# Down projection of a hybrid encoder's feed-forward layer: 18 of 22 inner tiles by seven products instead of 12, and the last 512 tokens finished in two parts

## The chip, the cores and the metric

The kernel runs on one core of one Trainium2 chip. The metric is the device time of one execution in microseconds; several executions are timed, and their median counts. One further execution was taken with the hardware profiler, and all rows quoted below come from it. The engines are TensorE (PE, with its weight loads as PEld), VectorE (DVE), ScalarE (ACT), GpSimd (POOL) and SyncE (SP), which issues most of the DMAs.

## What is computed

One layer of an encoder on 1024 tokens of width 1024, in float32: two token mixers side by side, then a gated feed-forward layer, then a final RMSNorm. The change concerns the end:

```python
def _conv_glu_ffn(h, w_up, dw_w, dw_b, w_down):
    up = jnp.einsum("bsd,df->bsf", h, w_up)
    gate, val = jnp.split(up, 2, axis=-1)
    gate = _dwconv_centred(gate, dw_w, dw_b)
    return jnp.einsum("bsf,fd->bsd", jax.nn.silu(gate) * val, w_down)
...
x = x + _conv_glu_ffn(h2, ...)
...
return _rmsnorm(x, final_norm_w)
```

The inner width is 2816, that is 22 tiles of 128. The down projection multiplies a matrix of 1024 tokens x 2816 by one of 2816 x 1024.

## The kernel before

**Layout.** Activations lie with channels on the 128 partitions and tokens along them. A page is 128 x 512 float32: one tile of 128 channels for one half (512) of the tokens. An output column tile `i` (0 to 7) has two pages, `xr[i][0]` and `xr[i][1]`.

**A product in full precision** (`mm3`, lines 142 to 150) is three matmuls: every operand is split (`split`, line 122) into a high part, cast by ScalarE, and the rest, subtracted by VectorE (both appear as line 124 in the profile); high x high, high x low and low x high are added up in PSUM. Lines 148, 149 and 150 are these three.

**Seven products** (`pair_job`): two output tiles (`i` and `i + 4`) x two token halves are a 2 x 2 block of a product whose inner tiles are also taken as two halves of `NS` = 3. Such a block takes seven products of `NS` inner tiles instead of eight, with sums of operands and of weights as inputs. The sums of activations (four per pair of inner tiles, `g_sums`) are made in the up stage and stored in `d_gc`; the sums of weights are either made in the job by four additions (`plus`, line 312) or made ahead once in `down_sums` (line 1945), stored in `d_ws` and read back. A job of seven products runs in the order 1, 2, 6, 7, 5, 4, 3; each product is issued in two steps, so a job has 14 steps (`per_seven`). After products 1, 6 and 7 `take` (line 1807) adds what `xr` held; after 2, 5, 4 and 3 `f` in `seven_evac` (line 1811) writes the new value of one page.

**Stages of the down projection.** `FIRST` = 6 inner tiles go through plain jobs (`std_down`), one job per output tile, two halves each, two inner tiles a step, 6 steps a job; ScalarE copies the result into `xr` (line 1797). Then `SEVENS` = 2 groups of 6 inner tiles by seven products, four jobs each. In the last group, when a page gets its final value of that group, POOL issues a DMA that adds the residual `d_x2` onto it (line 1814). Then the 4 remaining inner tiles (`LAST0` and up) in 16 plain jobs (`last_jobs`), all eight tiles for the first 512 tokens, then all eight for the last 512. After each, VectorE adds the result to `xr` (line 1869) and `turn_out` is issued four steps later: TensorE turns the page into token order, four blocks of 128 x 128 (line 1882), ScalarE takes squares with their sum (line 1884), VectorE multiplies by the gain into a separate tile `y` (line 1893). When all eight tiles of a half are there, the sums are reduced (1889), scaled (1890) and raised to -1/2 by POOL (1891), and `scale_out` multiplies each block of 128 tokens by its factor, 640 columns on VectorE (1917) and 384 on ScalarE (1914), and stores it (1920).

**Order.** TensorE runs in program order, which is written out by hand. `run_jobs` yields after each step; a job's weights are prepared one job ahead by a generator that pauses for a number of steps (`yield 4` and so on) between loads and splits; whatever is not ready when a product needs it is issued at that point. `later(n, do)` issues `do` after `n` further steps. The other engines and queues are ordered by a planner, but for instructions marked `pin`, which stay behind all that was issued before them on their engine. `fill_to(n)` runs steps up to number `n`; the lists `at` say at which step each operand of the next group is loaded (`load_seven`, line 1760; it is split four steps later). Operands take two pages out of 48 (`hx`, 32, and `gx`, 16) in turn, a group of seven needs 42. PSUM has three banks `mm`, two `sc`, two `tr` and one `ob`. Loaded weights pass through `wr` (two buffers, line 135) into `wp` (four).

The up stage before it (`ffn_job`) also runs by seven products; after each inner tile `gated` makes the gated value and stores it in `d_g`.

Of the kernel before, what the change touches and what calls it, by code (L numbers as in the profile page):

```python
# [30 lines left out]
BASE_STEPS = 1  # L31
H = 512
# [15 lines left out]
def tile_hybrid_encoder(  # L48
# [500 lines left out]
    def scratch(name, *dims):  # L549
# [1055 lines left out]
    ffn_order = [*range(FIRST), *in_pairs, *range(LAST0, NF)]  # L1605
    b12_only = in_pairs[::2]
# [18 lines left out]
    def ffn_job(n):  # L1625
# [3 lines left out]
        def gated(hf):  # L1629
# [146 lines left out]
    for half in range(2):  # L1776
# [4 lines left out]
    advance_chores(1 << 10)  # L1781
# [4 lines left out]
    xr = [[page(fd, "xr", 2 * ND) for _ in range(2)] for _ in range(ND)]  # L1786
    fnw = fd.tile([P, D], F32, name="fnw")
    nc.sync.dma_start(
        fnw, bass.AP(tensor=final_norm_w.tensor, offset=final_norm_w.offset, ap=[[0, P], [1, D]])
    )  # L1790
# [4 lines left out]
    def first_evac(i):  # L1795
# [3 lines left out]
        return f  # L1799

    def seven_evac(i, last):
# [7 lines left out]
        def f(e, half, x0, x1=None, op=ALU.add):  # L1809
            t = out_of(e, half)  # L1810
            V.tensor_tensor(t, x0, t if x1 is None else x1, op=op)
            if last:
                o = i + e * ND // 2
                G.dma_start(t, d_x2[o][half], accum_op=ALU.add)
# [11 lines left out]
    def seven_down(s):  # L1826
# [18 lines left out]
        return [job(i) for i in range(ND // 2)]  # L1845

    def last_jobs(f0, evac):

        kept = {}

        def job(i, half):
            def prep():
                if i not in kept:
                    raw = raw_w(w_cols(ffn_w_down, f0 * P, 4, i * P), 4)
                    pages = [g_page().rearrange("p (k e) -> p k e", k=4) for _ in range(2)]
                    kept[i] = split(*pages, raw, V)
                return kept[i]

            return prep, std_job(None, 4, lambda k, h: gs[f0 + k, h], evac(i), (half,), 1)[1]

        return [job(i, half) for half in range(2) for i in range(ND)]

    y_tags = itertools.cycle(["tr", "sc"])

    def final_evac(i):


        def f(half, acc):
            V.tensor_tensor(xr[i][half], acc, xr[i][half], op=ALU.add)
            later(4, lambda: turn_out(i, half))  # L1870

        return f

    def turn_out(i, half):

        t = xr[i][half]
        if i == 0:
            out_y.append(fy.tile([P, 4, D], F32, tag="y", name=nm("y"), bufs=2))
        ss, y = out_ss[half], out_y[half]
        b = bank(next(y_tags))  # L1880
        for c in range(4):
            T.transpose(b[:, c * P : (c + 1) * P], t[:, c * P : (c + 1) * P], ident)
        for c in range(4):
            A.activation(
                out_junk[c % 2], b[:, c * P : (c + 1) * P], AF.Square, accum_out=ss[:, i, c : c + 1]
            )
        if i == ND - 1:
            rs = cp.tile([P, 4], F32, name=nm("frs"), tag="frs", bufs=2)
            V.tensor_reduce(rs, ss.rearrange("p i c -> p c i"), axis=AX.X, op=ALU.add)
            V.tensor_scalar(rs, rs, 1.0 / D, EPS, op0=ALU.mult, op1=ALU.add)  # L1890
            G.tensor_tensor(rs, rs, mhalf.to_broadcast([P, 4]), op=ALU.pow)
            out_r.append(rs)
        gain = V.tensor_tensor(
            y[:, :, i * P : (i + 1) * P],
            b.rearrange("p (c e) -> p c e", c=4),
            view(fnw, i * P, [[0, 4], [1, P]]),
            op=ALU.mult,
        )
        if i == ND - 1:
            pin(gain)  # L1900

    def finish(half):
        for c in range(4):
            if half == 0:
                later(2 * c + 3, lambda c=c: scale_out(half, c))
# [3 lines left out]
    def scale_out(half, c):  # L1909
        y, rs = out_y[half], out_r[half]  # L1910
        for o, cols in ((0, 640), (640, D - 640)):
# [117 lines left out]
```

## Time and profile before

| | |
|---|---|
| runs | 1744.45, 1746.06, 1745.98 us |
| median | 1745.98 us |
| profiled execution | 1742.35 us |
| its span, first to last instruction | 1740.5 us |
| TensorE busy in the span | 98% |
| VectorE, ScalarE, POOL busy | 72%, 48%, 10% |
| moved by DMA | 308.26 MB, 177 GB/s |

In rows of the time order the columns are start in us, duration in us, engine, line, operation, output <- inputs, partitions x elements, number of instructions merged, and in brackets the idle time before it and what ended it. In rows of groups they are line, engine, operation, names, shapes, number | busy us, mean ns of one | idle us before, by releaser. `SPq` is the queue of DMA issues on SyncE. Matmuls are pipelined: the duration shown of one is longer than the time from its start to the next.

### The profile page before, as it was taken

The page shows a single profiled execution, that of the slowest core. Times are in us where ns is not written, and L with a number is a line of the kernel's source. Part 1 is how long each engine was busy: PE and PEld are TensorE (multiplying, and loading weights), DVE is VectorE, ACT ScalarE, POOL GpSimd, SP SyncE. Part 2 cuts the span into 40 slices and gives each one's busy share as a digit, 9 for nine tenths or more (in the row PEclk, how much of TensorE's full clock was granted, in tenths as well). Part 3 has the DMA queues.
Part 4 walks back from the last instruction along what each step waited for, and adds up shares of the span by engine and source line. Part 5 has one row for each costly group of instructions (what it writes and reads, how often), then busy time and mean ns, then how long its engine had stood idle before and what let it go on. Part 6 is the DMA issues. An engine that isn't in the chain of part 4 may idle for free. (4 is left out here: it accounts for less than half of the span.)

```text
span 1740.5 us, 30439 instructions
## 1 busy us (share of the span) xinstructions
PE 1711.8 (98%) x11806; PEld 1409.4 (81%) x11806; DVE 1254.2 (72%) x1919; ACT 828.0 (48%) x1544; POOL 170.2 (10%) x184
## 2 busy tenths in 40 slices
PE   8999999999999999999999999999999999999997
PEld 6878888887888888888878887888888888888775
DVE  4599999746678888787556467667767776657864
ACT  7444433334476777776342245444334434443333
POOL 2211111100000000000000002011111111000110
PEclk9999999999999999999999999999999999999999
DMA  8768888855663444446589466577777776783842
GB/s 284 241 169 186 198 189 195 210 162 159 211 202 108 126 131 126 126 120 202 176 257 329 140 206 193 146 146 167 157 167 160 180 170 152 230 264 109 202 91 97
DMA packets 343750, 308.26 MB, mean 177 GB/s; under 512 B 25262, under 2 KB 255798, under 8 KB 343606
## 3 DMA queue, kind: packets, MB, share of 16 engines
q1 hardware_dynamic: 289590, 267.51, 49.0%
q0 software_dynamic: 44800, 37.76, 15.2%
q10 hardware_dynamic: 9216, 1.05, 0.4%
q8 instruction: 92, 1.51, 0.4%
q14 instruction: 52, 0.43, 0.1%
HBM read 201.40 MB, written 87.03 MB: 166 GB/s over the span
## 5 line engine op out<-in xcount | busy, mean ns | idle before, releaser
L148 PE MATMUL mm<-hx,wp 128*128 128x512 f32 x1068 | 427.3, 400 | 3.3 <-ACT tm L849 1.4
L150 PE MATMUL mm<-hx,wp 128*128 128x512 f32 x1068 | 417.1, 391 | 0.9 <-DVE wp L124 0.9
L149 PE MATMUL mm<-hx,wp 128*128 128x512 f32 x1068 | 416.6, 390 | 0.4 <-DVE hx L124 0.4
L124 ACT CAST wp<-wr 128x1024 fp32r<-128x1024 f32 (+2 forms) x147 | 147.2, 1002 | 258.6 <-PE mm L149 112.5
L148 PEld LDWEIGHTS mm<-hx,wp 128*128 128x128 f32 x1068 | 200.6, 188 | 46.7 <-DVE ev L798 2.2
L150 PEld LDWEIGHTS mm<-hx,wp 128*128 128x128 f32 x1068 | 200.4, 188 | 45.1 <-DVE wp L124 2.4
L149 PEld LDWEIGHTS mm<-hx,wp 128*128 128x128 f32 x1068 | 200.8, 188 | 40.5 <-DVE hx L124 1.2
L124 DVE TENSOR_TENSOR wp<-wr,wp 128x1024 fp32r<-128x1024 f32 (+2 forms) x145 | 169.5, 1170 | 67.3 <-ACT wp L124 61.0
L1037 DVE SCALAR_TENSOR_TENSOR acc<-gl,v_b,acc 128x1024 f32<-128x1024 f32 x120 | 149.2, 1282 | 0.4
L1142 DVE TENSOR_TENSOR qF<-qF,tb 128x512 f32<-128x512 f32 x96 | 65.1, 686 | 21.0 <-ACT A L1174 20.9
L439 ACT COPY su<-mm 128x512 f32<-128x512 f32 x82 | 47.5, 579 | 59.2 <-PE mm L150 58.9
L124 ACT CAST wq<-sw 128x1024 fp32r<-128x1024 f32 x41 | 43.1, 1052 | 59.5 <-PE mm L149 44.6
L148 PE MATMUL tr<-hx,wp 128*128 128x512 f32 x180 | 70.5, 392 | 0.0
L150 PE MATMUL tr<-hx,wp 128*128 128x512 f32 x180 | 70.1, 389 | 0.0
L149 PE MATMUL tr<-hx,wp 128*128 128x512 f32 x180 | 70.0, 389 | 0.0
L1634 DVE SCALAR_TENSOR_TENSOR tm<-gp,v_a,tm 128x512 f32<-128x512 f32 x88 | 66.0, 750 | 3.9 <-ACT tm L1632 2.0
L1142 DVE TENSOR_TENSOR kG<-kG,tb 128x512 f32<-128x512 f32 x96 | 65.3, 686 | 3.7 <-PE sc L1279 3.6
L148 PE MATMUL mm<-hy,wp 128*128 128x512 f32 x164 | 64.5, 393 | 0.0
L148 PE MATMUL sc<-hy,wq 128*128 128x512 f32 x164 | 64.3, 392 | 0.0
L149 PE MATMUL mm<-hy,wp 128*128 128x512 f32 x164 | 64.3, 392 | 0.0
L150 PE MATMUL sc<-hy,wq 128*128 128x512 f32 x164 | 64.2, 391 | 0.0
L149 PE MATMUL sc<-hy,wq 128*128 128x512 f32 x164 | 63.8, 389 | 0.0
(372 smaller groups left out, 3577.6 us busy)
## 6 DMA issues: line engine op xcount, KB each, us to landing
wr<-in_w_in_dram SPq DMA_DIRECT2D x48, 512.0 KB, 4.7
wr<-in_ffn_w_up_dram SPq DMA_DIRECT2D x22, 512.0 KB, 4.0
sw<-in_w_in_dram SPq DMA_DIRECT2D x38, 256.0 KB
d_g<-ft SPq DMA_DIRECT2D x38, 256.0 KB, 3.4
sw<-in_ffn_w_up_dram SPq DMA_DIRECT2D x38, 256.0 KB, 4.4
sw<-in_ffn_w_up_dram POOLq DMA_DIRECT2D x19, 512.0 KB, 8.1
wr<-sw POOLq DMA_DIRECT2D x32, 256.0 KB, 3.6
wr<-wr POOLq DMA_DIRECT2D x32, 256.0 KB, 4.0
```

The source lines that it names most:

```text
L124: parts = A.copy(hi, src), eng.tensor_tensor(lo, src, hi.bitcast(F32), op=ALU.subtract)
L148: T.matmul(acc, whi[:, k, :], ahi, start=first, stop=False, skip_group_check=again)
L149: T.matmul(acc, whi[:, k, :], alo, start=False, stop=False, skip_group_check=again)
L150: T.matmul(acc, wlo[:, k, :], ahi, start=False, stop=last, skip_group_check=again)
L439: A.copy(t, acc)
L1037: V.scalar_tensor_tensor(acc, g[:, k : k + S], tap(k), acc, op0=ALU.mult, op1=ALU.add)
L1142: V.tensor_tensor(o, a, b, op=op)
L1634: V.scalar_tensor_tensor(c, g[:, o + k : o + k + H], vec("fdw", k * NF + j), c, op0=ALU.mult, op1=ALU.add,)
```

## The change

The constants become `FIRST` = 4, `SEVENS` = 3, and the plain last tiles go. The third group does output tiles 0, 1, 2 and 4, 5, 6 by seven products; tiles 3 and 7 are done by plain jobs over its six inner tiles, the first 512 tokens at once, the last 512 in two parts of 256. The pages of tiles in the third group are turned as soon as they have their value, within the group, and the gained values go back into the page that held them (now parts of one tile `x_out[half]` each). The residual is added in four batches during the first group. Stored weight sums are for the first two jobs of the third group only. Loads are placed by one sorted list `plan`.

```diff
+STORED = ((2, 0), (2, 1))
...
-    FIRST, NS, SEVENS = 6, 3, 2
-    LAST0 = FIRST + 2 * NS * SEVENS
+    FIRST, NS, SEVENS = 4, 3, 3
     d_ws = {
-        si: dp.tile([P, 4, NS * P], F32, name="d_ws_%d_%d" % si) for si in ((0, 0), (0, 3), (1, 0))
+        si: dp.tile([P, 4, NS * P], F32, name="d_ws_%d_%d" % si) for si in STORED
     }
...
-    ffn_order = [*range(FIRST), *in_pairs, *range(LAST0, NF)]
-    b12_only = in_pairs[::2]
+    ffn_order = [*range(FIRST), *in_pairs]
+    b12_only = in_pairs[: 2 * NS * (SEVENS - 1) : 2]
...
-            if hf and FIRST <= j < LAST0:
+            if hf and j >= FIRST:
...
-    xr = [[page(fd, "xr", 2 * ND) for _ in range(2)] for _ in range(ND)]
+    x_out = [fd.tile([P, ND, H], F32, name=nm("xo")) for _ in range(2)]
+    xr = [[x_out[half][:, i, :] for half in range(2)] for i in range(ND)]
...
+    def residual(i):
+        for o in (i, i + ND // 2):
+            for half in range(2):
+                G.dma_start(xr[o][half], d_x2[o][half], accum_op=ALU.add)
...
             if last:
                 o = i + e * ND // 2
-                G.dma_start(t, d_x2[o][half], accum_op=ALU.add)
+                later(3, lambda: turn_out(o, half, range(4), "mm" if (e, half) == (1, 0) else "ob"))
...
-        return [job(i) for i in range(ND // 2)]
+        return [job(i) for i in range(ND // 2 - (s == SEVENS - 1))]
...
+    PARTS = [(0, range(4)), (1, range(2)), (1, range(2, 4))]
+    def last_jobs(f0):
+        tiles = ND // 2 - 1, ND - 1
+        def operand(k, half):
+            if half == 0:
+                return gs[f0, 1 + k // NS, k % NS]
+            return gs[f0 + k, 1] if k < NS else gs[f0, 3, k - NS]
+        def job(i, half, chunks):
+            cols = slice(chunks[0] * P, (chunks[-1] + 1) * P)
+            def steps(w):
+                raw = raw_w(w_cols(ffn_w_down, f0 * P, 2 * NS, i * P), 2 * NS)
+                yield 5 if i < ND // 2 else 3
+                w[0] = split(w_page(2 * NS), w_page(2 * NS), raw, V, True)
...
+                acc = bank("mm")[:, cols]
+                for k in range(2 * NS):
+                    act = [part[:, cols] for part in operand(k, half)]
+                    mm3(acc, w, act, k, k == 0, k == 2 * NS - 1)
+                    yield
+                t = xr[i][half][:, cols]
+                V.tensor_tensor(t, acc, t, op=ALU.add)
+                later(4, lambda: turn_out(i, half, chunks, next(y_tags)))
+        return [job(i, *part) for part in PARTS for i in tiles]
...
         gain = V.tensor_tensor(
-            y[:, :, i * P : (i + 1) * P],
+            t[:, o : o + n].rearrange("p (c e) -> p c e", e=P),
...
     def scale_out(half, c):
+        y = fy.tile([P, D], F32, tag="y", name=nm("y"), bufs=6)
+        r = out_r[half, c]
+        for i, m in ((0, 5), (5, 3)):
+            src = x_out[half][:, i : i + m, c * P : (c + 1) * P]
...
         if s == 0:
-            at = [12 + 2 * n for n in range(12)] + [starts[0] - 8 + n // 2 for n in range(6)]
-            at += [starts[0] - 5 + n for n in range(3)]
+            at = [8 + 4 * n // 3 for n in range(15)] + [starts[0] - 3 + n for n in range(3)]
+            at += [starts[0] + 1 + 2 * n for n in range(3)]
...
+    plan.append((starts[0] + 24, 1, lambda: load_gain))
+    for i, n in enumerate((18, 32, 60, 68)):
+        plan.append((starts[0] + n, 1, lambda i=i: lambda: residual(i)))
+    for k in range(NS):
+        at = starts[SEVENS - 1] + per_seven + 6 * k
+        plan.append((at, 4, lambda k=k: load_g(f0 + k, 1)))
+    for n, delay, do in sorted(plan, key=lambda p: p[0]):
+        fill_to(n)
+        later(delay, do())
...
+    fill_to(starts[SEVENS] + per_half + 3)
+    finish(*PARTS[0])
+    fill_to(starts[SEVENS] + 2 * per_half + 5)
+    finish(*PARTS[1])
     st.drain()
     advance_chores(1 << 10)
-    finish(1)
+    finish(*PARTS[2], late=False)
```

`turn_out`, the reduction and `finish` now take the blocks of 128 tokens they are to treat, so that each of the three parts has its own factors. The gain of the final norm is loaded during the first group instead of ahead of the stage. In place of one flush of pending work at the end of the up stage there is a loop, since the last pair's sums are now issued by work that is itself pending there.

More of the change, by code (lines that the diff above doesn't have):

```diff
@@ L1780, in tile_hybrid_encoder @@
     s_ffn.drain()
-    advance_chores(1 << 10)
+    while chores:
+        advance_chores(1 << 10)
     fu.release()
@@ L1863, in tile_hybrid_encoder, with run @@
[L1863 to L1883, printed above, removed]
+            def run(parts):
+                w = parts[0]
+                acc = bank("mm")[:, cols]
[6 more added lines that the diff above has]
+                later(4, lambda: turn_out(i, half, chunks, next(y_tags)))
```

108 lines of the change are left out of this document (53 added, 55 removed).

## Prediction

> **What bounds the kernel now.** I read the page's totals first, then the busy time by stretch of the down projection, then the order of time on VectorE, ScalarE, the SP queue and TensorE in those stretches.
>
> ```profile
> span 1740.5 us, 30439 instructions
> PE 1711.8 (98%) x11806; PEld 1409.4 (81%) x11806; DVE 1254.2 (72%) x1919; ACT 828.0 (48%) x1544; POOL 170.2 (10%) x184
> ...
> 1460.00:1480.00 20.00, 20.00 (x89) 16.38 (x88) 14.37 (x19) 9.90 (x15) 3.35 (x3) 1.00 0.56 112
> 1480.00:1500.00 20.00, 20.00 (x89) 16.38 (x88) 19.23 (x30) 12.55 (x22) 0.00 (x0) 1.00 0.76 247
> 1500.00:1520.00 20.00, 20.00 (x90) 16.57 (x89) 9.36 (x14) 7.43 (x13) 0.00 (x0) 1.00 0.71 215
> 1520.00:1540.00 20.00, 20.00 (x90) 16.53 (x90) 11.02 (x18) 8.14 (x16) 0.00 (x0) 1.00 1.03 306
> 1540.00:1562.00 22.00, 22.00 (x99) 18.22 (x98) 10.28 (x15) 12.45 (x22) 0.00 (x0) 1.00 0.71 230
> 1606.00:1621.00 15.00, 15.00 (x68) 12.43 (x67) 14.87 (x25) 10.27 (x18) 0.00 (x0) 1.00 0.83 267
> 1621.00:1635.00 14.00, 13.17 (x57) 10.28 (x56) 12.22 (x20) 4.42 (x7) 3.19 (x4) 1.00 0.92 244
> ...
> 1678.00:1690.00 12.00, 11.61 (x55) 8.89 (x54) 5.86 (x9) 4.75 (x21) 0.33 (x1) 1.00 0.58 149
> ```
>
> Columns of the stretches: length, busy us of PE, PE weight loads, DVE, ACT, POOL, granted clock, DMA share, GB/s. TensorE is busy in every stretch but two: 0.83 us are open in 1621:1635, just after the second group of seven begins, and 0.39 us in 1678:1690, where the last stage begins. So a matmul less is its time gained, and a new wait of TensorE is its time lost. DVE is full twice, in 1480:1500 and 1606:1621 (14.87 of 15): there nothing more is free.
>
> What a matmul costs is its distance to the next, not its duration. Two rows of the time order of DVE, the last evacuation of two jobs of seven products that follow each other, are one job apart; two rows of ACT's, the second-half copy of two plain jobs, likewise:
>
> ```profile
> 1633.18 0.69 DVE L1811 TENSOR_TENSOR xr<-mm,xr 128x512 f32<-128x512 f32 x1 [1.35 <-PE mm L150]
> 1647.46 0.69 DVE L1811 TENSOR_TENSOR xr<-mm,xr 128x512 f32<-128x512 f32 x1 [1.35 <-PE mm L150]
> ...
> 1504.28 1.05 ACT L1797 COPY xr<-mm 128x512 f32<-128x512 f32 x2
> ...
> 1515.48 0.59 ACT L1797 COPY xr<-mm 128x512 f32<-128x512 f32 x1 [2.99 <-PE mm L150]
> ...
> 1523.64 0.59 ACT L1797 COPY xr<-mm 128x512 f32<-128x512 f32 x1 [2.47 <-PE mm L150]
> ```
>
> 14.28 us over 7 x 3 x 3 = 63 matmuls, and 8.16 us over 6 x 2 x 3 = 36, are both 0.2267 us.
>
> **Matmuls (-6.1 us).** Before: plain stage 6 x 8 x 2 x 3 = 288, two groups 2 x 4 x 63 = 504, last stage 4 x 8 x 2 x 3 = 192, together 984. After: plain 192, full groups 504, third group 3 x 63 = 189, last stage 6 tiles x 2 columns x 2 halves x 3 = 72 in widths of 512, together 957. 27 x 0.2267 = 6.1 us. The turns number 64 as before; 48 of them only move into the third group.
>
> **Narrow matmuls (+0.1 us; 0 to +8.1).** The second half of the last stage runs as 72 matmuls of 256 columns. None stands in the trace. The nearest rows are products of 128 columns, merged two by two:
>
> ```profile
> 603.27 0.39 PE L1368 MATMUL ob<-Sf,qF 128*128 128x128 f32 x2
> 603.50 0.39 PE L1368 MATMUL ob<-Sb,qF 128*128 128x128 f32 x2
> ```
>
> 0.23 us for two: some 0.115 us each, almost exactly half of 0.2267, though each has its own weight load. I take 0.115, against 0.113 for half a wide one: 72 x 0.002 = 0.1 us. At the other end a narrow one costs as much as a wide one, 72 x 0.113 = 8.1 us. The Trainium skill, "TensorE: Matmul & The Clock Gate", Part 3 (what overlaps and what doesn't), says that a weight load runs beside a matmul in flight only where their row groups differ; all matmuls here use all rows, so by it the narrow ones would be no cheaper than wide ones and the sum would be 8 us worse, the second rival below. The trace speaks against it: loads are busy 81% of the span beside a PE at 98%.
>
> **The end (-3.3 us; -4.5 to -1).** From the start of the last matmul to the end of the span, all engines in order of time, then the output's row among the DMA issues:
>
> ```profile
> 1727.09 0.39 PE L150 MATMUL mm<-hx,gx 128*128 128x512 f32 x1
> ...
> 1727.52 0.69 DVE L1869 TENSOR_TENSOR xr<-mm,xr 128x512 f32<-128x512 f32 x1 [0.83 <-PE mm L150]
> ...
> 1728.36 0.63 PE L1882 MATMUL sc<-ident,xr 128*128 128x128 f32 x4 [0.44 <-DVE xr L1869]
> ...
> 1730.01 0.22 ACT L1884 ACTIVATION_READ_ACCUMULATOR oj<-sc 128x1 f32 x1
> 1730.26 0.21 DVE L1889 TENSOR_REDUCE frs<-os 128x4 f32<-128x32 f32 x1 [0.38 <-ACT oj L1884]
> ...
> 1730.75 1.01 POOL L1891 TENSOR_TENSOR frs<-frs,mhalf 128x4 f32<-128x4 f32 x1 [22.44 <-DVE frs L1890]
> ...
> 1731.79 1.94 DVE L1917 TENSOR_SCALAR y<-y,frs 128x640 f32<-128x640 f32 x4 [0.53 <-POOL frs L1891]
> ...
> 1732.43 2.88 SPq L1920 DMA_DIRECT2D out_dram<-y  x4
> ...
> out_dram<-y SPq DMA_DIRECT2D x8, 512.0 KB, 5.1
> ```
>
> 1740.5 - 1727.1 = 13.4 us. After, with half the columns and counted from the last narrow matmul: the addition starts at 0.43 and takes some 0.4 (0.69 for twice the width); two turns end at 1.3; two squares of 0.25 and a read of 0.2 at 2.0; reduction, scaling and power (1730.26 to 1731.76, 1.5 us) at 3.6; the first of two scalings gives its store at 4.25, the second at 4.8; 5.1 us to landing give 9.9. The scaling of the part before may stand ahead on DVE for 0.2: 10.1, against 13.4. The eight stores together are 4.19 MB and wait for nothing but their scalings, so the last one could also stand behind the six others; that is the -1 end.
>
> **First plain halves (+0.5 us; 0 to +1.7).** A plain half now takes 12 x 0.2267 = 2.72 us, not 4.08, and the three `mm` banks cover 8.16 us instead of 12.2. The first two copies ran at 1504.28 (x2 above), behind the gating of the last up tile. The second half of job 0 ended one half before 1507.3, so the stage began near 1495.0 and the fourth half wants its bank at 1503.2: 1.7 us short, if the copy comes no earlier. It should come earlier: eight operands are split at the end of the up stage, not twelve, and DVE is what was full there; four splits (row below) are 2.7 us.
>
> ```profile
> L124 DVE TENSOR_TENSOR hx<-tm,hx 128x512 fp32r<-128x512 f32 x20 | 13.4, 685 | 0.8 <-ACT hx L124 0.7
> ...
> 1627.02 0.55 DVE L312 TENSOR_TENSOR sr<-sr,sr 128x384 f32<-128x384 f32 x1
> 1627.49 0.55 DVE L312 TENSOR_TENSOR sr<-sr 128x384 f32<-128x384 f32 x1
> ...
> 1564.44 0.69 DVE L1811 TENSOR_TENSOR xr<-tr,su 128x512 f32<-128x512 f32 x1 [0.48 <-PE tr L150]
> 1565.08 0.96 DVE L124 TENSOR_TENSOR wp<-sr,wp 128x768 fp32r<-128x768 f32 x1
> ```
>
> **Start of the first group (+1.35 us; 0 to +1.4).** Its first weights are no longer read as stored sums. They are prepared from step 26; with pauses of 4, 2, 4 and 3 steps their product 6 would be split at step 39, but product 6 starts at step 37, so the split is issued there, pinned on DVE behind the evacuation after product 2. The last two rows above are that spot before: the evacuation at 1564.44 could start only as product 2 ended, a split behind it runs 1565.08 to 1566.04, and TensorE wants the low part with the third matmul of product 6, at 1564.0 + 3 x 0.23 = 1564.69. 1566.04 - 1564.69 = 1.35 us.
>
> **Group borders (+2.7 us; +0.8 to +4.5).** Before there is one border, with 0.83 us open and DVE full. After there are two. At the first, the weights of job (1,0) are no longer stored sums: four additions, 0.47 us apart by the rows above, 1.9 us on a full DVE. At the second they are stored, as in the border before: 0.8 us.
>
> **Last stage (0).** The 0.39 us open at its start, where raw weights were late, go: it needs two weight tiles, not eight. I set the same against it for the weights of the second tile, split three steps before their use.
>
> **Hidden.** In the up stage three more pairs get four sums each: 12 x 0.69 = 8.3 us of DVE (same width as the addition at 1727.52) and twelve stores. Cover: DVE does 14.37 of 20 us in 1460:1480 beside a full PE; without cover, those 8.3 us. The last pair's fall in 1506 to 1509, in the half-idle DVE of 1500:1520. The residual's 16 adding transfers move from the last group to the first, on POOL, with at least 30 us before the next use of their pages:
>
> ```profile
> L1814 POOL DMA_DIRECT2D xr<-d_x x16: 859/859/864, 1624.0 to 1677.5; - x16
> ...
> DMA to landing us min/median/max: 3.5/4.3/5.8
> ```
>
> **Transfers in the plain stage (0; 0 to +12).** The stretches 1500:1562 moved 20 x 215 + 20 x 306 + 22 x 230 = 15.5 MB. Away go 1.0 (weights of two inner tiles), 1.6 (a third set of sums), 0.5 (the gain), 0.6 (first group's weights); 1.05 come (last pair's sums): 12.8 MB, while the stage shrinks from 65.3 to 43.5 us. At the 306 GB/s seen that is 42 us. The last operands are wanted only some 10 us into the group, so even the mean of 250 GB/s (51 us) would do. I take 0.
>
> **Sum.** -6.1 + 0.1 - 3.3 + 0.5 + 1.35 + 2.7 = -4.75 us: the profiled span 1740.5 becomes 1735.7. That execution took 1742.35, 1.85 over its span and 3.6 under the median shown; set against the median 1745.98, the forecast is 1741.2.
>
> **Rivals.**
>
> Full gain: the new waits don't come. The planner places the first group's split earlier and DVE catches up at the borders; the wait terms (4.55) vanish: -9.3, 1736.7. For: at the old border a full DVE cost only 0.83. Against: the pins, and no free DVE there.
>
> Narrow matmuls cost as much as wide ones: -4.75 + 8.0 = +3.3, 1749.2. For: the loads alone are long, 81% of the span. Against: the rows of 128 columns.
>
> The plain stage becomes bound by transfers and their queue: slower. SP issues in order, and it stood still behind a store of sums that waited for DVE, with a plain weight load behind it:
>
> ```profile
> 1507.57 2.36 SPq L1939 DMA_DIRECT2D sr<-in_ffn_w_down_dram  x3
> 1517.08 1.52 SPq L1947 DMA_DIRECT2D d_ws<-sr  x2
> ...
> 1519.18 0.62 SPq L135 DMA_DIRECT2D wr<-in_ffn_w_down_dram  x1
> ```
>
> 7 us of standing fitted into 8.16 us jobs and do not fit into 5.44 us ones. If the mix moves only 230 GB/s as in 1540:1562, 12.8 MB take 55.7 us: 12.2 late, +7.4, 1753.4. It decides slower below 12.8 MB / (43.5 + 4.75 us) = 265 GB/s, if all of it is wanted by the stage's end. Against: 306 GB/s was reached.
>
> It does not do what it says: the pages of each half are now one tile, and a wait could be made for all of it. Then each batch of four adding transfers (4 x 0.86 + 4.3 = 7.7 us, less some 2 of slack) holds the evacuations: 4 x 5.7 = 23 us, 1764. Against: above, four scalings of one `y` tile ran back to back from 1731.79 while its first store, issued at 1732.43, was still reading.
>
> **How the numbers follow.** Forecast 0.52, own range 1738 to 1744.5; full gain 0.16; narrow 0.07; transfers 0.17; one tile 0.04; 0.04 for others. A measurement of this kernel tells a change from none at about 0.2%, 3.5 us: faster is below 1742.5. Full gain and four fifths of the forecast's chance lie there: 0.16 + 0.42, with a little of others 0.59; same 0.22 (the rest of the forecast, most of narrow, the mild end of transfers); slower 0.19. Range 1735 to 1751: it leaves out one tile and the far end of transfers.
>
> **What would show it.** Some 957 wide-equivalents and 72 matmuls of 256 columns about 0.115 us apart; 10 us from last matmul to end; a gap of about 1.3 us at the first group's product 6, and 2.7 and 0.8 us at the two borders, ended by DVE; no gap in the plain stage with wr loads as releaser. I am wrong if the plain stage is longer than 46 us, if narrow starts are 0.2 us apart, or if TensorE waits for turned pages in the third group.

## The result: the time after, and the profile after

Over five runs the changed kernel takes 1751.98 us (1750.41 to 1753.5) against 1744.56 us (1742.87 to 1746.06) for the kernel before on the same chip: a ratio of 1.0034, 95% interval [1.0021, 1.0048]. It is slower by 0.3%; the forecast was 4.75 us faster. The profiled execution took 1750.41 us.

Totals of the page of after, then its busy time by stretch (columns as in the prediction):

```profile
span 1748.6 us, 30615 instructions
PE 1710.0 (98%) x11815; PEld 1406.7 (80%) x11815; DVE 1285.4 (74%) x1976; ACT 838.1 (48%) x1562; POOL 170.5 (10%) x185
```

```profile
1500.00:1520.00 20.00, 16.05 (x68) 12.96 (x67) 10.86 (x17) 8.57 (x15) 0.00 (x0) 0.95 0.86 272
1520.00:1540.00 20.00, 20.00 (x87) 16.49 (x86) 11.84 (x20) 10.75 (x20) 0.00 (x0) 0.97 0.98 315
```

TensorE was busy all through 1500:1562 before; now 4 us are open in 1500:1520, while VectorE does only 10.86 us in it, and the granted clock is 0.95 and 0.97. Gaps of 1 to 2 us follow at the start of the first group and at its end. What TensorE waited for from the up stage on (us in total, times, longest):

```profile
PE mm L151 <- DVE wp L125: 8.7, 5, 3.9
PE sc L1903 <- DVE xo L1890: 2.4, 2, 1.2
PE sc L149 <- DVE su L1816: 1.1, 1, 1.1
PE mm L149 <- ACT su L440: 1.1, 1, 1.1
PE mm L149 <- DVE su L1816: 0.8, 1, 0.8
PE ob L599 <- POOL tm L619: 0.7, 1, 0.7
```

All but two end with VectorE. (The one on `tm` L619 is there before the change too, as long. The one on `su` L440, in the up stage, comes and goes between executions of one kernel; so below the *stretch* is compared, from the start of the last matmul of the up stage to the end of the span.) Before it was 1740.5 - 1494.64 = 245.9 us, after 1748.6 - 1497.24 = 251.4: +5.5, with 2.6 us more ahead of it. The gaps in the order of TensorE, with the matmul that ends each:

```profile
1514.03 0.39 PE L150 MATMUL mm<-hx,wp 128*128 128x512 f32 x1
1518.36 0.80 PE L151 MATMUL mm<-hx,wp 128*128 128x512 f32 x1 [3.95 <-DVE wp L125]
1518.95 0.63 PE L149 MATMUL mm<-hx,wp 128*128 128x512 f32 x1
1519.38 0.63 PE L150 MATMUL mm<-hx,wp 128*128 128x512 f32 x1
...
1552.83 0.50 PE L151 MATMUL mm<-hx,wp 128*128 128x512 f32 x1 [1.51 <-DVE wp L125]
...
1557.59 0.50 PE L149 MATMUL mm<-gx,wq 128*128 128x512 f32 x1 [0.80 <-DVE su L1816]
...
1604.10 0.47 PE L149 MATMUL sc<-gx,wq 128*128 128x512 f32 x1 [1.10 <-DVE su L1816]
...
1614.78 0.50 PE L151 MATMUL mm<-hx,wp 128*128 128x512 f32 x1 [1.80 <-DVE wp L125]
...
1673.39 0.50 PE L151 MATMUL mm<-hx,wp 128*128 128x512 f32 x1 [1.20 <-DVE wp L125]
...
1734.87 0.44 PE L1903 MATMUL sc<-ident,xo 128*128 128x128 f32 x2 [1.14 <-DVE xo L1890]
```

From 1514.03 to 1518.36 are 4.33 us, of which 0.23 are a matmul's own distance: 4.10 lost, in the fourth plain job. Of the next six distances the first is 0.59 us and five are 0.43, where the usual distance is 0.2267: 1.37 us more.

Why that split was late shows in the time order of the engines, rows of SP's queue, VectorE and ScalarE:

```profile
1506.38 2.63 SPq L1614 DMA_DIRECT2D d_gc<-ft  x4
1509.06 0.49 SPq L1760 DMA_DIRECT2D tm<-d_g  x1
1509.63 1.33 SPq L1970 DMA_DIRECT2D sr<-in_ffn_w_down_dram  x2
...
1505.66 2.87 DVE L1613 TENSOR_TENSOR ft<-ft,ft 128x512 f32<-128x512 f32 x4
1516.09 0.56 DVE L1976 TENSOR_TENSOR sr<-sr,sr 128x384 f32<-128x384 f32 x1 [7.56 <-DMA sr<-in_ffn_w_down_dram]
...
1517.62 0.68 DVE L125 TENSOR_TENSOR wp<-wr,wp 128x512 fp32r<-128x512 f32 x1
...
1508.33 0.62 ACT L125 CAST wp<-wr 128x512 fp32r<-128x512 f32 x1 [1.91 <-PE mm L150]
```

VectorE stands idle for 7.56 us in front of the first addition of stored weight sums (`down_sums`), whose raw weights were issued only at 1509.63, behind the four stores of the last activation sums. The cast of the fourth job's plain weights was done at 1508.95 (the casts of the third, fourth and fifth job start at 1502.89, 1508.33 and 1513.82, their splits at 1503.55, 1517.62 and 1523.23). The split that belongs to it was ready from then on; it stands behind three of the additions and runs at 1517.62. TensorE wanted it at 1514.26.

### The profile page after: what moved, and what is told of

Same layout as the page of the kernel before. It is cut to its first block, busy times and chain, and to the rows that moved or that the text cites. A ratio compares the mean times of both kernels' runs of the same rounds, so it can differ in the third digit from the quotient of the medians.

```text
span 1748.6 us, 30615 instructions
## 1 busy us (share of the span) xinstructions
PE 1710.0 (98%) x11815; PEld 1406.7 (80%) x11815; DVE 1285.4 (74%) x1976; ACT 838.1 (48%) x1562; POOL 170.5 (10%) x185
## 5 line engine op out<-in xcount | busy, mean ns | idle before, releaser
L149 PE MATMUL mm<-hx,wp 128*128 128x512 f32 x1086 | 434.9, 400 | 4.6 <-ACT tm L849 1.5
L151 PE MATMUL mm<-hx,wp 128*128 128x512 f32 x1086 | 424.5, 391 | 9.1 <-DVE wp L125 9.1
L150 PE MATMUL mm<-hx,wp 128*128 128x512 f32 x1086 | 423.4, 390 | 0.4 <-DVE hx L125 0.4
L151 PEld LDWEIGHTS mm<-hx,wp 128*128 128x128 f32 x1086 | 204.3, 188 | 56.0 <-DVE wp L125 12.8
L149 PEld LDWEIGHTS mm<-hx,wp 128*128 128x128 f32 x1086 | 204.4, 188 | 49.7 <-DVE ev L798 3.1
L150 PEld LDWEIGHTS mm<-hx,wp 128*128 128x128 f32 x1086 | 204.5, 188 | 40.6 <-DVE hx L125 1.2
L125 DVE TENSOR_TENSOR wp<-wr,wp 128x1024 fp32r<-128x1024 f32 (+1 forms) x147 | 169.0, 1150 | 64.4 <-ACT wp L125 63.8
L149 PE MATMUL tr<-hx,wp 128*128 128x512 f32 x197 | 77.4, 393 | 0.0
L151 PE MATMUL tr<-hx,wp 128*128 128x512 f32 x197 | 76.7, 389 | 0.0
L150 PE MATMUL tr<-hx,wp 128*128 128x512 f32 x197 | 76.7, 389 | 0.0
L440 ACT COPY su<-mm 128x512 f32<-128x512 f32 x82 | 47.5, 579 | 55.9 <-PE mm L151 55.6
```

The lines of the kernel that those rows point to most:

```text
L125: parts = A.copy(hi, src), eng.tensor_tensor(lo, src, hi.bitcast(F32), op=ALU.subtract)
L149: T.matmul(acc, whi[:, k, :], ahi, start=first, stop=False, skip_group_check=again)
L150: T.matmul(acc, whi[:, k, :], alo, start=False, stop=False, skip_group_check=again)
L151: T.matmul(acc, wlo[:, k, :], ahi, start=False, stop=last, skip_group_check=again)
L440: A.copy(t, acc)
```

## The experiments

Thirteen variants of the kernel after, the later ones built on earlier ones, and both kernels once more.

### No stored weight sums

```diff
-STORED = ((2, 0), (2, 1))
+STORED = ()
```

> The changed kernel without any stored weight sums: the two sets of additions and their 3.1 MB in the plain stage go, and the third group's first two jobs make their sums themselves. Theory A (TensorE loses time where VectorE, in order, stands at additions whose raw weights have not landed, with a plain weight split queued behind): the wait at the start of the fourth plain job (4.1 us before one matmul, and some 1.4 us of slower matmuls after it) goes, and the border into the third group gets longer by the four additions, from 1.4 to about 3.3 us; the time falls by some 3.5 us. Theory B (the plain stage is bound by how much the DMA engines move): 3.1 MB fewer shorten the stage likewise, so this run alone does not tell the two apart. Theory C (the new waits are spread over the borders and do not hang on the sums): nothing changes by more than 1 us.

Measured: stretch 248.2 (-3.2); 1747.65 us, 1.0013 [1.0001, 1.0025] of before. The plain stage has no gap; the split stands right behind its cast:

```profile
1510.95 2.87 DVE L1613 TENSOR_TENSOR ft<-ft,ft 128x512 f32<-128x512 f32 x4
1514.27 0.69 DVE L125 TENSOR_TENSOR wp<-wr,wp 128x512 fp32r<-128x512 f32 x1 [0.44 <-ACT wp L125]
```

In return the second border, whose sums are now made in it, has distances of 1.48, 2.18 and 0.74 us in place of one of 1.58. So `down_sums` costs the 5.4 us in the plain stage and saves some 2.4 at the second border.

### The loads and stores of the sums without their additions

This kernel leaves the eight additions out and stores unsummed weights in their place, so that DMA traffic and queue stay.

```diff
-            for t, a, b in ((c0, r0, o0), (c1, o0, o1), (r0, r0, c1), (r1, r1, r0)):
-                V.tensor_tensor(t, a, b, op=ALU.add)
-            for to, t in zip(sums_of(d_ws[s, i], NS), (col, rows)):
+            for to, t in zip(sums_of(d_ws[s, i], NS), (other, rows)):
```

> The changed kernel with the loads and the stores of the weight sums kept, byte for byte, but without the eight additions between them (the third group's first two jobs then read unsummed weights; left out is the summing). Theory A: the wait at the fourth plain job goes as in the run without stored sums, 5.5 us, and the border into the third group stays at 1.4 us; the time falls by 5 us. Theory B: the bytes are the same, so the wait stays within 1 us of 4.1 us and the time with it.

Measured: stretch 248.7 (-2.6); 1748.7 us, 1.0015 [1.0002, 1.0028]. The 4.1 us wait is gone, as the order on VectorE would have it, but two smaller ones come (distances of 1.03 and 1.33 us, on the copies `xo` L1801), and behind the next at product 6 eight matmuls are 0.43 apart. ScalarE's rows at the first of them, and SP's queue before it:

```profile
1522.26 0.62 ACT L125 CAST wp<-wr 128x512 fp32r<-128x512 f32 x1 [6.50 <-DMA wr<-in_ffn_w_down_dram]
1522.79 0.58 ACT L1801 COPY xo<-mm 128x512 f32<-128x512 f32 x1
...
1512.08 2.43 SPq L1976 DMA_DIRECT2D d_ws<-sr  x2
1514.56 0.43 SPq L1970 DMA_DIRECT2D sr<-in_ffn_w_down_dram  x1
1515.42 0.36 SPq L1976 DMA_DIRECT2D d_ws<-sr  x1
1515.87 0.44 SPq L136 DMA_DIRECT2D wr<-in_ffn_w_down_dram  x1
```

Casts that wait for late plain weights hold the copies that empty the banks. The weights are late because SP issued them (1515.87) behind three stores (line 1976), the last two of which stood there until the raw weights that they store had landed. So both are real: VectorE's order cost the 4.1 us, and behind it stood SP's queue of transfers, good for about 2 us. That the span before this stretch is the same as in the kernel before (up stage 414.3 us in both) shows the extra activation sums hidden.

### The first group's weights prepared four steps earlier

```diff
-            if st.count == starts[0] - 2 * per_std + 2:
+            if st.count == starts[0] - 2 * per_std - 2:
```

> The weights of the first group's first job are prepared from step 22 instead of 26. The prediction's reading of the gap at product 6 (1.7 us, the low part is split behind the evacuation after product 2): the gap goes, all else stays, the span falls by 1.5 us. Rival: VectorE is late there because the plain stage ran late, so the gap stays or moves to the next product.

Measured (one execution, 1751.77 us): the gap before product 6 (1.90 us) is gone and nothing stands in its place. The stretch is only 0.7 us shorter, 250.7, since the plain stage's wait, as a distance, came to 4.46 us and 14 matmuls after it, not 6, were slow. The gap was indeed the place of the split.

### The first two parts scaled later

```diff
-    fill_to(starts[SEVENS] + per_half + 3)
+    fill_to(starts[SEVENS] + per_half + 10)
     finish(*PARTS[0])
-    fill_to(starts[SEVENS] + 2 * per_half + 5)
-    finish(*PARTS[1])
     st.drain()
+    finish(*PARTS[1], late=False)
```

> The scaling of the first 512 tokens is issued seven steps later and that of the next 256 after the last addition. If the two waits in the last stage (1.3 us at the turn of the second part, 1.4 us at the end) come from scalings that stand ahead of the additions on VectorE, both shrink to under 0.5 us and the span falls by 1 to 2 us. Rival: the end is set by the stores, eight of 0.5 MB on one queue, and later scalings make them later: no gain, or up to 1 us lost.

Measured (one execution, 1754.65 us): the wait at 1733 is gone, one of 1.25 us stays, and the last matmul to the end takes 10.7 us, after 10.5. No gain: the scaling only moves. What stands in the way is its size:

```profile
1732.03 2.45 DVE L1946 TENSOR_SCALAR y<-xo,frs 128x640 f32<-128x640 f32 x3 [0.55 <-POOL frs L1918]
1734.40 0.41 DVE L1890 TENSOR_TENSOR xo<-mm,xo 128x256 f32<-128x256 f32 x1
```

These are rows of the kernel after: 0.82 us for a scaling of five tiles, 640 columns in runs of 128, where four contiguous ones took 1.94 before, 0.485 each. The addition that empties the last stage's bank stands behind three of them, and the turn behind the addition (1734.87 above).

### The weight sums made in the output projection

The same two sets, made at an earlier stage: `halves_of` moves up, and `down_sums` goes.

```diff
+    todo += [(*halves_of(*si), NS, d) for si, d in d_ws.items()]
...
-        s_o.fill(16 if n else 8)
+        s_o.fill(10 if n else 8)
...
-    for n, si in enumerate(d_ws):
-        plan.append((1 + 4 * n, 4, lambda si=si: down_sums(*si)))
```

> The same two sets of weight sums, but made in the output projection before the up stage, beside the three sets that are made there already, and not in the plain stage. Counted from the last matmul of the up stage to the end of the span: before 245.9 us, changed kernel 251.4. Theory A (additions with late loads ahead of a plain weight split on VectorE): the plain stage has no wait over 0.5 us, the border into the third group keeps its 1.4, and this stretch is 245.5 to 246. Theory B (transfers bound the plain stage): it is 3.1 MB lighter and so the same, but the output projection pays by more than 1 us. Theory C (the loss is in the borders, whatever is done with the sums): over 249.

Measured: stretch 247.1 (-4.3); 1746.1 us, 1.0003 [0.9991, 1.0015]. No gap in the plain stage, and the short second border (1.59) is kept. The 1 us missing is a slow spell of seven matmuls at the first border.

### Sums for the first border too

The kernel of the last run, with a third set:

```diff
-STORED = ((2, 0), (2, 1))
+STORED = ((1, 0), (2, 0), (2, 1))
```

> As the run with the sums in the output projection, with the sums of the second group's first job stored as well. If the waits at the first border (1.25 us before product 5 of the last job of the first group and 1.95 us at the second group's first low part) come from the four additions on a full VectorE, together 1.9 us, the first border costs 1.4 us like the second, and the stretch falls by another 1.8 us to about 244. Rival: the border is bound by the casts and loads of the 18 operands, the same in both, and does not move.

Measured: stretch 247.0; 1745.71 us, 1.0 [0.999, 1.0011]. The four additions are out of the first border, and it is no shorter:

```profile
1608.89 0.47 PE L149 MATMUL mm<-hx,wp 128*128 128x512 f32 x1 [0.86 <-DVE su L1817]
...
1611.47 0.50 PE L151 MATMUL mm<-hx,wp 128*128 128x512 f32 x1 [1.87 <-DVE wp L125]
```

### The combination

The last kernel with the earlier preparation and the final scaling shared four tiles to VectorE, four to ScalarE, and no longer five to three:

```diff
-        for i, m in ((0, 5), (5, 3)):
+        for i, m in ((0, 4), (4, 4)):
```

> As the run with the border's sums stored, with the first group's first weights prepared four steps earlier and the final scaling halved between VectorE and ScalarE (512 columns each, not 640 and 384). The gap of 1.7 us at product 6 of the first job goes, the two waits of the last stage fall from 1.2 and 1.3 us to about 0.7 each: the stretch is 241 to 242 us, 4 us under the kernel before, and the median about 1742. Rival: the waits that go reappear in the next place where VectorE is full, and the stretch stays over 243.

Measured: stretch 240.9; 1742.1 us (1738.61 to 1745.46), 0.9977 [0.9963, 0.9991] of before: faster than both kernels. Its waits:

```profile
PE mm L151 <- DVE wp L125: 3.3, 3, 1.9
PE sc L1904 <- ACT y L1945: 1.0, 1, 1.0
PE mm L149 <- DVE su L1817: 0.8, 2, 0.5
```

### The last half in one part

```diff
-    PARTS = [(0, range(4)), (1, range(2)), (1, range(2, 4))]
+    PARTS = [(0, range(4)), (1, range(4))]
...
-    fill_to(starts[SEVENS] + 2 * per_half + 5)
-    finish(*PARTS[1])
...
-    finish(*PARTS[2], late=False)
+    finish(*PARTS[1], late=False)
```

> The changed kernel with the last 512 tokens finished in one part (36 wide matmuls for 72 narrow ones, four blocks of 128 tokens at the end). If the two parts are worth what the prediction says, the time from last matmul to end rises from 10.5 to some 13.4 us; the wait of 1.2 us at the turn of the second part goes, so the stretch from the last stage's start to the end is about 1.5 us longer. Rival: the additions' wait behind scalings eats the whole gain, and the stretch is no longer than in the changed kernel.

Measured (one execution, 1754.58 us): the last matmul starts at 1737.82 and the span ends at 1752.7, 14.9 us against 10.5 in two parts. From the last wait for weights (1723.55; after 1722.24) to the end are 29.15 us against 26.36: two parts are worth 2.8 us, even with narrow matmuls and more waits on VectorE. Here a full-width addition stands behind a late scaling of the part before, and the turn waits 2.01 us for it.

### The first border: three runs with the residual moved

All three start from the combination and pin the adding transfers on POOL behind what was issued before them.

```diff
-                G.dma_start(xr[o][half], d_x2[o][half], accum_op=ALU.add)
+                pin(G.dma_start(xr[o][half], d_x2[o][half], accum_op=ALU.add))
...
-    for i, n in enumerate((18, 32, 60, 68)):
+    for i, n in ((0, 18), (2, 20), (3, 22), (1, 32)):
```

The second run has `((0, 18), (3, 20), (1, 32), (2, 46))`, the third `((3, 68), (2, 73), (0, 79), (1, 89))`.

> The run with all repairs, with the residual's 16 adding transfers kept out of the first border: those of output tiles 2, 3, 6 and 7 are issued on POOL right behind the first four, before their jobs instead of after them, and stay in program order. In the run before this one four to six of them ran in the 20 us before the first border (DMA share 1.08 there), ScalarE waited three times for operands there, and storing the border's weight sums had not shortened it. Theory D (the transfers make the operands late): the first border costs no more than the second, 1.4 us instead of 2.5, the DMA share before it stays under 0.9, and the stretch from the last up-stage matmul to the end falls from 240.9 to about 239.7 us. Theory E (a full VectorE alone, with the weight split queued behind operand splits): the first border stays at 2.5 us and the stretch with it.

Measured: the first border has one distance of 1.58 us, like the second. But stretch 246.4; 1749.71 us, 1.0026 [1.0015, 1.0036]: eleven transfers in a row on POOL, and the next job's additions wait for their raw weights:

```profile
1558.34 9.73 POOL L1809 DMA_DIRECT2D xo<-d_x  x11 [10.05 <-ACT wq L125]
...
1583.15 0.56 DVE L313 TENSOR_TENSOR sr<-sr,sr 128x384 f32<-128x384 f32 x1 [6.03 <-DMA sr<-in_ffn_w_down_dram]
...
1584.09 0.69 DVE L1817 TENSOR_TENSOR su<-mm,xo 128x512 f32<-128x512 f32 x1
```

TensorE lost 5.5 us to it, until the evacuation at 1584.09. It is the plain stage's mechanism again: additions whose loads are late, with an evacuation in line behind them.

> The kernel of the combination (two sets of sums moved, inputs of product 6 prepared earlier, final scaling in equal halves), with the residual of the tiles of one job of the first group, tiles 3 and 7, moved from the first border to the stretch behind that job's own pass, instead of all of them right behind the first as in the run before. Theory (the first border is long because the adding transfers of the residual share it with the operand loads): the border's long wait of 2.27 us falls to 1.6 or less with half of the transfers gone, no wait of over 1 us appears in the middle of the group, and the time from the last matmul of the up stage to the end is about 239.8 us (240.88 in the combination); the ratio to before 0.997. Rival (any adding transfers inside the group make the raw weights of the next job late, as the twelve in a row did): a wait of over 1 us ahead of product 5 or 7 in the middle of the group, and the stretch is 241 us or more, ratio 0.998 or worse.

Measured: stretch 243.9; 1744.89 us, 1.0004 [0.9988, 1.002]. No gap in the middle of the group, but a longer border: distances of 2.52 and 2.26 us and seven slow matmuls, though the last adding transfer was issued by 1587.24. Neither side had this.

> The kernel of the combination, with all sixteen adding transfers of the residual moved from the first group to the middle of the second group (four batches, at 12, 17, 23 and 33 steps after its start), so that the first border and the stretch ahead of it hold none at all. Theory (the first border is long because the adding transfers fill the DMA engines beside its operand loads: share 1.08 and 0.97 in 1590:1604 of the two runs with a long border, 0.84 and 0.82 in borders with a short one): DMA share in the first border is 0.85 or less, its waits become those of the second, one of about 1.6 us, and the time from the last matmul of the up stage to the end is about 239.7 us (240.88 in the combination); ratio to before about 0.997. Rival (the border is long for another reason, the order of its operand loads or splits): two waits with 2.2 us or more in the longer one stay with no transfer beside them; the stretch is 240.9 us or more. A price may show in the second group: raw weights late behind the transfers, a wait of over 1 us in 1615:1650.

Measured: stretch 246.0; 1748.74 us, 1.0012 [0.9999, 1.0025]. The planner let the transfers run ahead of the steps named: one went out at 1592.84, eight from 1605.41 on. Up to that point the border held one transfer, and it is as long as with all of them:

```profile
1606.22 0.47 PE L149 MATMUL mm<-hx,wp 128*128 128x512 f32 x1 [0.36 <-DVE su L1817]
...
1608.80 0.50 PE L151 MATMUL mm<-hx,wp 128*128 128x512 f32 x1 [1.88 <-DVE wp L125]
```

Its stretch 1592:1608 still has a DMA share of 0.98. The price came as named: a distance of 2.28 us in the second group, with nine slow matmuls. So the transfers ahead of the border do not make it long. VectorE worked without a gap from 1600.91 on, and the split that ended the wait (1607.79) stands behind operand splits and an evacuation, not behind a load. That the border was short in the first of the three runs goes with the 5.5 us that TensorE had stood there some 20 us before; whether the loads used that lead was not tried. Why the first border is longer than the second stays open.

### Five tiles or six in the final scaling

In the combination four tiles took 0.43 us each, less than the contiguous 640 columns, so the runs of 128 alone are not what makes five slow. Two runs let VectorE scale six, ScalarE two: the kernel after with this edit alone, and the combination with it.

```diff
-        for i, m in ((0, 5), (5, 3)):
+        for i, m in ((0, 6), (6, 2)):
```

> The kernel after with one edit: of the eight tiles of the final scaling VectorE takes six and ScalarE two, in place of five and three. VectorE's scaling took 0.82 us for five strided tiles (640 columns), 0.43 us for four strided tiles (512 columns, in the combination) and 0.485 us for 640 contiguous columns in the kernel before. Theory A (it is the odd number of tiles, not the stride, that makes five slow; an even number is read at twice the rate): six tiles, though more, take 0.43 + 2 x 0.058 = about 0.54 us each; the addition behind three scalings starts 0.8 us earlier, the two waits of TensorE (1.32 and 1.39 us) shrink by about 0.7 us each, and the stretch is 1.5 us shorter, about 249.9. Theory B (the runs of 128 are slow, with a threshold in size): six tiles take 0.96 us or more, the waits grow by 0.3 to 0.4 us, and the stretch is 252 us or more.

Measured, the kernel after with six tiles: 0.56 us each, less than five took.

```profile
1732.18 1.68 DVE L1946 TENSOR_SCALAR y<-xo,frs 128x768 f32<-128x768 f32 x3 [0.56 <-POOL frs L1918]
1733.78 0.42 DVE L1890 TENSOR_TENSOR xo<-mm,xo 128x256 f32<-128x256 f32 x1
```

And four, in the combination:

```profile
1723.81 1.28 DVE L1947 TENSOR_SCALAR y<-xo,frs 128x512 f32<-128x512 f32 x3 [0.55 <-POOL frs L1919]
1725.00 0.42 DVE L1891 TENSOR_TENSOR xo<-mm,xo 128x256 f32<-128x256 f32 x1
```

So 0.43, 0.82 and 0.56 us for four, five and six tiles: theory A. Of the two waits of the last stage the first fell as expected, from 1.31 to 0.54 us, the last did not (1.60, before 1.39). The stretch is 250.8, 0.6 less and not 1.5, and no gain shows in the time: 1751.47 us, 1.0045 [1.0031, 1.0059].

> The combination with the same edit: VectorE takes six tiles of the final scaling and ScalarE two, in place of four and four. Theory A (even numbers are fast): VectorE's scaling goes from 0.43 to 0.54 us, ScalarE's from 0.67 (1.33 for two) to about 0.45; the last wait of TensorE, on ScalarE's scaling, 1.0 us, shrinks by 0.4, the end by 0.3: stretch about 240.5, ratio to before 0.997. Theory B (size with runs of 128): VectorE's scaling takes 0.96 us or more, the additions stand behind it again, stretch 242.5 us or more.

Measured: 0.56 us a scaling again, but the last wait is 1.42 us, now on VectorE, where it was 1.0 on ScalarE with four and four; with a longer first border (2.97 and 1.91 us, and eight slow matmuls) the stretch is 245.3. 1742.24 us, 0.9989 [0.9979, 0.9999]: faster than before, but no better than the combination.

### Both kernels once more

> The kernel before, profiled once more. From the start of the up stage to its last matmul it took 414.3 us; runs of the changed kernel and its variants took 414.3 to 419, with one to three waits of TensorE for a copy on ScalarE that stands behind a cast whose raw weights land late. If that is chance of an execution and not the change, this execution too may take more than 414.3; the stretch after the up stage stays at 245.9 within 0.5 us. If it is the change, both are as before.

> The changed kernel, profiled once more. The wait at the fourth plain job is there again, 4 us within 0.5, and the stretch after the up stage takes 251.4 within 1 us; the up stage may take anything from 414.3 to 419.

One execution each: before 1747.64 us with a stretch of 247.2, 0.8 over the upper end of what was expected, after 1750.77 us with 252.4. The wait in the plain stage repeats, a distance of 4.87 us with ten slow matmuls, and so does the difference of the stretches, 5.2 us. The up stage took 418.0 us before, and not 414.3 again, and 415.7 after, where it was 416.0: its waits come and go with either kernel. Two executions of one kernel also differ by 1.0 and 1.3 us in the stretch, so less than that between single executions of two variants shows nothing.

## Why the prediction was wrong, point by point

The starts of TensorE's instructions give the account of the stretch. Every distance of more than 0.17 us over the usual one counts as a wait.

| term | forecast, us | measured, us |
|---|---|---|
| 27 matmuls fewer | -6.1 | -6.1 |
| 72 narrow matmuls | +0.1 | +0.8 |
| the end, from the last matmul | -3.3 | -2.9 |
| plain stage: first halves | +0.5 | 0 |
| plain stage: transfers, sums | 0 | +5.47 (4.10, then 1.37 at the slow spacing) |
| first group: product 6 | +1.35 | +1.67 |
| first group: additions of its second job | 0 | +0.95 |
| two borders, 0.8 forecast and 1.17 measured before | +2.7 | +3.4 (1.25 + 1.96 + 1.35 - 1.17) |
| last stage, 0.39 forecast and 0.71 measured before | 0 | +1.0 (0.42 + 1.31 - 0.71) |
| sum | -4.75 | +4.3 |

Measured in the stretch are +5.5; the other 1.2 us lie in distances too small to be told apart one by one. Of the 10.25 us between forecast and stretch over half is one line. The medians differ by 7.4 us; the part that the stretch does not hold, some 2 us, lies ahead of it, where two executions of the kernel before differ by 4 us (the up stage's last matmul at 1494.64 and at 1498.63), and its cause stays open.

**The step that failed** is "Transfers in the plain stage", taken as 0. It set megabytes against time and found room. Bytes were not what decided. The stage took 49.1 us (1497.47 to 1546.61), past the 46 named as a sign of being wrong. The nearest rival, the plain stage bound by transfers and their queue at 1753.4 us, was right about the place, and nearly in the time, but not in the means: it had SP standing behind a store that waits for VectorE, and a rate under 265 GB/s, while the stretches moved 272 and 315. SP did stand so, from 1512.03 to 1517.14, but the weights for which TensorE waited had been cast since 1508.95; only in the run without additions did a plain load late in SP's queue cost something. What the runs show is VectorE standing in front of an addition whose raw weights are late, with a ready split in line behind it. Taking the additions and their loads away removed the wait, taking the additions alone removed it and showed the queue behind it (some 2 us), and making the same sums in an earlier stage removed it and kept their use. The forecast noted that 7 us of standing no longer fit into jobs of 5.44 us, and then gave that a chance of 0.17 without asking what is in line behind the additions on VectorE.

**The slow spell** after the wait, 1.37 us, was in no term. The profile has the granted clock at 0.50 for 3.41 us, from shortly before the wait ended:

```profile
1517.91:1521.32 3.41, 2.96 (x7) 2.38 (x8) 1.46 (x3) 0.00 (x0) 0.00 (x0) 0.50 1.02 324
```

By the Trainium skill, "TensorE: Matmul & The Clock Gate", Part 1 (The HAM clock gate), the clock falls to half after an idle window of about 3.4 us and comes back after as long a busy one, with matmuls of 512 columns 426.7 ns apart meanwhile. The wait of 4.1 us, the spacing of 0.43 us and the 3.41 us at half clock agree; in other runs the spell came after pauses of only 2 us (below). The wait was worth a third more than its length.

**Narrow matmuls** were right: they start 0.12 us apart, against 0.115 taken.

```profile
1727.15 0.28 PE L149 MATMUL mm<-gx,wp 128*128 128x256 f32 x1
1727.27 0.28 PE L150 MATMUL mm<-gx,wp 128*128 128x256 f32 x1
```

Over 72 of them, that and the wider distances beside turns make 0.8 us, a tenth of the rival's 8.

**The end** was right in size, 10.5 against 10.1; the last turn waits 1.22 us for its addition, behind two scalings of the part before, where 0.2 had been allowed. The run in one part shows that splitting the last half pays 2.8 us.

**Start of the first group** was right in place and cause (1.35 forecast, 1.67 measured); moving the preparation took it away. A second wait there was missed, again additions with late raw weights and an evacuation (L1816) behind them on VectorE:

```profile
1555.31 0.56 DVE L313 TENSOR_TENSOR sr<-sr,sr 128x384 f32<-128x384 f32 x1 [1.67 <-DMA sr<-in_ffn_w_down_dram]
...
1556.86 0.68 DVE L1816 TENSOR_TENSOR su<-mm,xo 128x512 f32<-128x512 f32 x1
```

**Borders**: near in sum, wrong in cause. The four additions blamed for the first border went in one run, and its length stayed. At the second border 1.35 us were lost, not 0.8; there stored sums do save what was expected of them, 2.4 us.

**Last stage** was taken as 0: its own weights cost only 0.42, but the scalings, 0.82 us instead of 0.485 each, stand ahead of its addition for 1.31. By the Trainium skill, "VectorE: DVE Perf Modes" (What auto-detection actually checks), an operation with one tensor source reads it through both ports, at twice the rate, only if the outermost dimensions of source and destination are both even, or equal. The source has 4, 5 or 6 tiles there, the destination is one row, and 0.43, 0.82 and 0.56 us agree with that.

**Hidden work** was right: with its added sums the up stage takes no more than 414.3 us where no wait falls into it, as in the run without additions.

## What to carry to other kernels

When a stage is made shorter, list for each engine what stands in line behind every instruction that waits for a DMA, and ask whether the shorter jobs still cover the lateness; bandwidth alone does not answer that. Work that is only preparation (sums of weights) belongs in a stage where its loads can be early: here the same sums, made in the output projection, made the difference between 1.0034 and 1.0003; with a third set and two small moves it came to 0.9977. Transfers in a long row should not go ahead of a load that an addition on the busy engine waits for.

## What the runs showed of the hardware that was not expected

After a pause of TensorE the next 6 to 14 matmuls could be 0.43 us apart, about twice the usual 0.2267, with a granted clock of 0.50 for 3.41 or 6.83 us. It came after pauses of 4 to 5 us, but also after one of 1.87 us at the first border of the run with three sets of sums, and not after an equal one at the same place of the combination. What differs is where the pause lies. Within one run the changes of the granted clock are whole multiples of 3.41 us apart. In the first run the pause lies in one such step, in which TensorE is busy for 1.45 us, and the step after it is at half. In the combination, with steps counted back from its change at 1731.54, the pause is divided between two, busy for 2.60 and 2.05 us:

```profile
1608.81:1612.22 3.41, 1.45 (x5) 0.96 (x6) 3.41 (x6) 1.70 (x4) 0.00 (x0) 1.00 1.06 279
1612.22:1615.63 3.41, 3.41 (x9) 2.64 (x9) 2.85 (x5) 0.88 (x2) 0.00 (x0) 0.50 1.08 328
...
1601.84:1605.25 3.41, 2.60 (x11) 1.54 (x9) 3.41 (x7) 2.59 (x4) 0.86 (x1) 1.00 1.09 293
1605.25:1608.66 3.41, 2.05 (x9) 1.72 (x10) 3.41 (x6) 1.77 (x3) 0.00 (x0) 1.00 1.08 303
```

Over all 17 traces, from 1300 us to the last stage, every one of the 16 steps at full clock in which TensorE was busy for 47% or less is followed by a step at half, and none with 56% or more is; of the six between, two are.

Twelve adding transfers of 256 KB, eleven of them issued in a row, brought the median landing of all sixteen to 11.2 us, from 4.8 when they were spread out.

A multiplication by one factor per partition took less time for six tiles of 128 columns (0.56 us) than for five (0.82).
